# Three seams and the tail of a decoder step's second half: pools for the output projection, gated weight loads, a last product in two halves

## The chip, the core and the metric

The kernel runs on one core of a Trainium2 chip. TensorE (PE) multiplies matrices into PSUM, VectorE (DVE) and ScalarE (ACT) work element by element, GpSimd (POOL) does small vector work here, and SyncE (SP) issues nearly all DMA transfers, in its program order. The metric is the device time of one execution in microseconds; less is better.

## The reference, cut to what matters

One decoder layer runs over 1024 prompt tokens and 64 tokens of eight decoding requests: two attention groups, an output projection, and an MLP, with a norm before and after each half.

```python
def rms_norm(x, g):
    xf = x.astype(jnp.float32)
    y = xf * lax.rsqrt(jnp.mean(xf * xf, axis=-1, keepdims=True) + NORM_EPS)
    return (y * g.astype(jnp.float32)).astype(x.dtype)
...
    mix = jnp.concatenate([o_diff, o_nsa], axis=-1) @ w_out
    x = x + rms_norm(mix, g_post_mix)
    hm = rms_norm(x, g_pre_mlp)
    ff = jnp.square(jax.nn.relu(hm @ w_up)) @ w_down
    x = x + rms_norm(ff, g_post_mlp)
```

`w_out` is 1024 x 1024, `w_up` 1024 x 4096, `w_down` 4096 x 1024, all in float32.

## The kernel before

All of it is one program whose instructions a scheduler puts in order on each engine; every engine then runs its list in that order. Tiles come from pools, memory areas that open and close like brackets; a tile that lies where a closed pool lay waits for that pool's last readers and writers. Each product is made of three fp32r products: a factor is split into a high part (`act_copy`, ACT, L138) and a low part (a subtraction on DVE, L1333 in `split2`), and high x high, low x high and high x low are added in PSUM.

**Differential attention** is the stage before. Its results go transposed to `mixT` in DRAM, one column block per tile of 128 tokens; the last head's last tiles end it.

**Output projection** (`phase_out`, L1232). Eight blocks of `w_out` are loaded into a ring of four tiles `ur` (L1240) and split into tiles `w` (L1245). Token tiles 0 to 7 and tile 8 (the 64 decoding tokens) then each go through `front` (load `mx` from `mixT` and `cx` from x, split `mx` into `mh`), `prod` (two halves of 24 matmuls into PSUM tiles `C`, L1271, three buffers) and `post` (norm, residual into `x1d`, second norm, eight transposes L1296 into `xf`). The pools of this phase are `xca`, `ur`, `w2`, `cc` and `cl` on the left and `xf` on the right.

**MLP up** (`phase_up`, L1366). Both MLP products use Strassen's scheme: seven products for four quarters, in the order `UORD`. `x_factor(i, p)` makes the seven x factors `xc` for each of two column halves p of the tokens (QT = 272 columns each); `factor(j, i)` makes the seven weight factors `us` for a block j. Per j, 168 matmuls (L1398) fill four PSUM tiles `Ua` to `Ud`; from them come seven blocks of h that are stored to `hF` in DRAM (L1418). The last four stores of a block need DVE sums of all its products.

**MLP down** (`phase_down`, L1492). `w_down` is four quarters q of 4 MB, each loaded in four chunks c (L1512). For each of seven factors in the order `DORD` and each of 16 blocks sb (112 steps n), `factor(n)` splits a weight block into `wf`, a block `hr` of `hF` into `hf`, and 24 matmuls (L1573) add into four tiles `Dn`. Four `hr` buffers are loaded ahead (L1506). `later` sets at which steps the chunks of quarters 1, 3 and 2 are issued. `done(i, db)` adds a finished product into the quarters `acc`.

**Finish** (`finish`, L1587). After the last product ten token tiles (five of each token half) are transposed back (L1597), squared and summed on ACT (L1598), scaled on DVE (L1600), added to `x1d` (L1603) and stored (L1608).

Of the kernel before, what the change touches and what calls it, by code (L numbers as in the profile page):

```python
# [17 lines left out]
F32 = mybir.dt.float32  # L18
# [28 lines left out]
DORD = (0, 6, 4, 5, 1, 3, 2)  # L47
# [77 lines left out]
class Kern:  # L125
# [1106 lines left out]
    def phase_out(self, cp, cl):  # L1232
# [5 lines left out]
        for k in range(KC):  # L1238
            raw = self.rp.tile([P, 4, 256], F32, name="ur", bufs=4).rearrange("p a n -> p (a n)")
# [6 lines left out]
            ws.append(w)  # L1246
        gpost = cl.tile([P, D], F32, name="gpost")
# [3 lines left out]
        xins, mhs, pss = {}, {}, {}  # L1251

        def front(t):
            m = self.tok(t)[2]
            xin = xins[t] = cp.tile([P, D], F32, name="cx", bufs=2)
            mx = cp.tile([P, KC, P], F32, name="mx", bufs=1)
            nc.sync.dma_start(mx[:, :, :m], self.mixT[:, t * P:t * P + m].rearrange("(k p) t -> p k t", p=P))
            nc.sync.dma_start(xin[:m], self.xsrc(t))
            mh = mhs[t] = cp.tile([P, 2, KC, P], FR, name="mh", bufs=2)
            self.act_copy(mh[:, 0, :, :m], mx[:, :, :m])  # L1260
            nc.vector.tensor_sub(mh[:, 1, :, :m], mx[:, :, :m], f32(mh[:, 0, :, :m]))
            pss[t] = []
# [41 lines left out]
        for t in range(NT - 1):  # L1304
            front(t)
# [60 lines left out]
    def phase_up(self, wp, tp, psU, close):  # L1366

        nc, A, rp = self.nc, self.A, self.rp
# [12 lines left out]
        def factor(j, i):  # L1381
# [4 lines left out]
            W[j, i] = w = wp.tile([P, 2, 4, P], FR, name="us", bufs=8)  # L1386
# [105 lines left out]
    def phase_down(self, qp, ap, fp, psD):  # L1492
# [5 lines left out]
        quarter, acc, F, R = {}, {}, {}, {}  # L1498
        quarter[0] = qp.tile([P, NB, 512], F32, name="q0")
        HB = 4  # L1500
        hr = [(i, sb) for i in DORD for sb in range(NB)]

        def load_h(n):
            i, sb = hr[n]
            R[n] = self.hp.tile([P, HT], F32, name="hr", bufs=HB)
            nc.sync.dma_start(R[n], self.hF[i, sb * P:sb * P + P])  # L1506

        def load_w(q, c):
            if q not in quarter:
                quarter[q] = qp.tile([P, NB, 512], F32, name=f"q{q}")  # L1510
            r, e = q % 2, q // 2
            nc.sync.dma_start(quarter[q][:, c * 4:c * 4 + 4], w_dn[e, :, c * 4:c * 4 + 4, r * 512:r * 512 + 512])  # L1512


        def factor(n):
            i, sb = hr[n]
            if n + HB < len(hr):
                load_h(n + HB)
            w = fp.tile([P, 2, 512], FR, name="wf", bufs=3)
            a11, a21, a12, a22 = ((quarter[q][:, sb] if q in quarter else None) for q in range(4))  # L1520
# [28 lines left out]
        later = {}  # L1549
        for k, (q, c) in enumerate([(q, c) for q in (1, 3, 2) for c in range(4)]):  # L1550
            later.setdefault(2 + (k % 4) * 4 + (k // 4) * NB, []).append((q, c))
        for c in range(4):
            load_w(0, c)
            load_h(c)
        for k in range(4):
            acc[k] = ap.tile([P, 4, HT], F32, name=f"acc{k}")
        for n in range(2):
            factor(n)
        first = list(range(0, NT, 2)) + [NT]
        for n, (i, sb) in enumerate(hr):  # L1560
            for q, c in later.get(n, ()):
                load_w(q, c)
# [359 lines left out]
```

## Time and profile before

| what | us |
|---|---|
| median of 3 runs | 1874.84 |
| lowest and highest run | 1874.23, 1878.4 |
| the profiled execution, own time | 1880.47 |
| its span, first to last instruction | 1878.7 |
| PE busy | 1717.1 (91% of the span) |
| DVE busy, ACT busy | 1140.6 (61%), 862.3 (46%) |

The profile has a page with shares of the span and of each of its 40 equal slices, a chain of the work that ended last, groups of instructions, and a timeline in which an instruction shows what ended the idle time before it. A busy matmul is a pipelined one, so the cadence of matmuls is read from long unbroken runs, not from the length of one.

### The profile page before, as it was taken

To read this page: it belongs to the slowest core of one execution; us is meant where nothing else is said; L and a number is where in the kernel's file an instruction comes from. 1 tells how busy PE (TensorE), PEld (TensorE's weight loads), DVE (VectorE), ACT (ScalarE), POOL (GpSimd) and SP (SyncE) were. 2 spreads that over 40 slices of the span, in tenths; PEclk is the share of its full clock that TensorE was granted. 3 is DMA by queue.
4 is the path that set the end of the run, shared out by engine and by line. 5 is a ranking of instruction groups with operands and counts; after the bars stand their busy time and mean duration, and the time that the engine had idled before them with its cause. 6 is when DMAs were issued, how large, how long until landed. Compare 5 with 4: busy or idle time off the path is not lost.

```text
span 1878.7 us, 33337 instructions
## 1 busy us (share of the span) xinstructions
PE 1717.1 (91%) x12155; PEld 1496.4 (80%) x12155; DVE 1140.6 (61%) x2673; ACT 862.3 (46%) x2168; POOL 280.5 (15%) x517
## 2 busy tenths in 40 slices
PE   6789999999999999999959969999999569999996
PEld 5778776776657787888747849999999469999995
DVE  4257767667754666666564576666665456448546
ACT  4254446556653555555453444444443224443333
POOL 1133335333321111111100100000000000000002
PEclk8899999999999999999989979999999779999997
DMA  8632000021102524333245304444432853333533
GB/s 167 120 83 47 17 12 21 6 79 51 30 8 58 158 69 138 87 89 112 59 127 174 133 23 128 146 145 138 151 133 104 322 191 91 96 106 91 176 91 110
DMA packets 191600, 191.92 MB, mean 102 GB/s; under 512 B 32291, under 2 KB 148619, under 8 KB 191435
## 3 DMA queue, kind: packets, MB, share of 16 engines
q1 hardware_dynamic: 190138, 187.51, 33.5%
q10 hardware_dynamic: 1296, 2.27, 0.5%
q8 instruction: 96, 1.57, 0.4%
q14 instruction: 70, 0.57, 0.1%
HBM read 133.75 MB, written 55.97 MB: 101 GB/s over the span
## 4 chain that ended last, share of the span: by engine, by line
PE 79%; DVE 6%; DMA 3%; issue 2%; SPq 2%; ACT 1%; POOL 1%; POOLq 0%; ACTq 0%; DVEq 0%
PE Dn L1573 17%; PE M L336 11%; PE C L1271 5%; PE S L409 5%; PE Ua L1398 5%; PE Ub L1398 5%; PE Uc L1398 5%; PE o L501 5%; PE T L516 4%; PE Ud L1398 2%; PE o L613 2%; SPq L1512 1%; PE S L1094 1%; PE o L1219 1%; PE S L336 1%
## 5 line engine op out<-in xcount | busy, mean ns | idle before, releaser
L1573 PE MATMUL Dn<-hf,wf 128*128 128x272 f32 x2688 | 344.4, 291 | 37.8 <-ACT hf L138 37.4
L1573 PEld LDWEIGHTS Dn<-hf,wf 128*128 128x128 f32 x2688 | 343.4, 192 | 38.7 <-ACT hf L138 38.1
L336 PE MATMUL M<-w,xt 128*128 128x384 f32 (+4 forms) x1584 | 296.0, 332 | 13.1 <-ACT nat L138 12.6
L336 PEld LDWEIGHTS M<-w,xt 128*128 128x128 f32 (+1 forms) x1584 | 247.6, 193 | 27.3 <-ACT nat L138 14.0
L426 ACT ACTIVATE p<-S,nm 128x512 f32<-128x512 f32 (+3 forms) x288 | 160.3, 562 | 102.3 <-DVE nm L421 55.5
L174 POOL TENSOR_TENSOR rs_r<-rs_t,mhalf 128x1 f32<-128x1 f32 (+2 forms) x64 | 45.2, 709 | 1011.6 <-DVE rs_t L172 976.8
L417 DVE TENSOR_REDUCE nm<-S 128x1 f32<-128x512 f32 (+3 forms) x288 | 148.1, 527 | 60.0 <-PE S L416 39.1
L409 PE MATMUL S<-kst,qs 128*128 128x512 f32 (+3 forms) x576 | 162.5, 375 | 6.3 <-ACT p L426 5.1
L138 ACT ACTIVATE wf<-q 128x512 fp32r<-128x512 f32 x112 | 70.7, 631 | 211.8 <-PE Dn L1573 196.3
L1333 DVE TENSOR_TENSOR wf<-q,wf 128x512 fp32r<-128x512 f32 x112 | 77.3, 691 | 149.2 <-ACT wf L138 149.1
L1271 PE MATMUL C<-w,mh 128*128 128x512 f32 (+1 forms) x432 | 104.2, 402 | 16.2 <-ACT mh L138 13.6
L480 POOL TENSOR_SCALAR p<-p,coef 128x640 f32<-128x640 f32 (+7 forms) x128 | 93.0, 741 | 146.0 <-DVE coef L477 83.3
L1398 PE MATMUL Ub<-xc,us 128*128 128x272 f32 x768 | 106.3, 291 | 6.4 <-ACT us L138 6.4
L1333 DVE TENSOR_TENSOR us<-ur,us 128x512 fp32r<-128x512 f32 x96 | 66.0, 691 | 74.5 <-ACT us L138 74.5
L1271 PEld LDWEIGHTS C<-w,mh 128*128 128x128 f32 (+1 forms) x432 | 80.2, 187 | 37.1 <-ACT mh L138 13.8
L409 PEld LDWEIGHTS S<-kst,qs 128*128 128x128 f32 x576 | 94.4, 196 | 18.1 <-ACT p L426 7.8
L1398 PE MATMUL Ua<-xc,us 128*128 128x272 f32 x768 | 104.0, 291 | 2.6 <-ACT us L138 1.1
L1398 PEld LDWEIGHTS Ub<-xc,us 128*128 128x128 f32 x768 | 100.8, 190 | 6.9 <-ACT us L138 6.7
L1398 PE MATMUL Uc<-xc,us 128*128 128x272 f32 x768 | 102.8, 289 | 1.9 <-DVE uh L1446 1.6
L1398 PEld LDWEIGHTS Ua<-xc,us 128*128 128x128 f32 x768 | 99.9, 190 | 3.4 <-ACT us L138 1.2
L1398 PEld LDWEIGHTS Uc<-xc,us 128*128 128x128 f32 x768 | 99.1, 189 | 2.4 <-DVE uh L1446 1.8
L138 ACT ACTIVATE us<-ur 128x512 fp32r<-128x512 f32 x96 | 59.9, 628 | 75.3 <-PE Uc L1398 48.4
(306 smaller groups left out, 3048.5 us busy)
## 6 DMA issues: line engine op xcount, KB each, us to landing
hr<-hF SPq DMA_DIRECT2D x112, 272.0 KB
hF<-uh SPq DMA_DIRECT2D x105, 272.0 KB
kvp<-cache_diff_kv SPq DMA_DIRECT2D x128, 128.0 KB
ur<-w_up SPq DMA_DIRECT2D x32, 512.0 KB
q<-w_down SPq DMA_DIRECT2D x16, 1024.0 KB
raw<-w_in SPq DMA_DIRECT2D x32, 192.0 KB
raw<-w_in SPq DMA_DIRECT2D x40, 128.0 KB
xin<-x_prompt SPq DMA_DIRECT2D x8, 512.0 KB
```

Of the source, the lines that this page charges most:

```text
L138: self.nc.scalar.activation(out, in_, AF.Copy, scale=scale)
L336: nc.tensor.matmul(ps[1][:m, :n], self.xt[c][:, a, k, c0:c0 + m], ws[k][:, b, :n], start=i == 0, stop=i == len(ops) - 1)
L409: nc.tensor.matmul(S[:, a * P - lo:b * P - lo], qs[:, ps, j, :], kst[hf][:, kc, a * P - lo:b * P - lo], start=ps == 0, stop=ps == 1 and no ...
L417: nc.vector.reduce_max(nm[:, n:n + 1], S[:, a * P - lo:b * P - lo], axis=AX.X, negate=True)
L426: nc.scalar.activation(p[:, a * P:b * P], tiles[n][:, a * P - lo:b * P - lo], AF.Exp, bias=nm[:, 0:1], accum_out=sums[:, n:n + 1])
L480: nc.gpsimd.tensor_scalar(v, v, coef[:, sw + 1, j:j + 1], 0.0, op0=OP.mult, op1=OP.add)
L501: nc.tensor.matmul(st["o"][half * 64:half * 64 + 64, pr * 256:pr * 256 + 256], lhsT, rhs, start=not started[half], stop=last, skip_group_c ...
L516: nc.tensor.transpose(T[:, m * 256 + jj * P:m * 256 + jj * P + P], st["p", sw, pr * 2 + jj][:, kb * P:(kb + 1) * P], self.ident)
L1271: nc.tensor.matmul(ps[:m], mhs[t][:, a, k, :m], ws[k][:, b, n * 512:n * 512 + 512], start=cnt == 0, stop=cnt == 3 * KC - 1)
L1333: lo.tensor_sub(w[:, 1], src, f32(w[:, 0]))
L1398: nc.tensor.matmul(ps[:, p, :QT], w[:, a, k, :], x[:, b, k, :], start=start and cnt == 0, stop=cnt == 11, skip_group_check=True)
L1573: nc.tensor.matmul(self.dps[db][:, p, :QT], w[:, a, db * P:(db + 1) * P], h[:, b, p * QT:(p + 1) * QT], start=sb == 0 and m == 0, stop=sb ...
```

## The change

**Projection.** The `ur` ring moves into a pool `rr` on the right side, where the last head's weights lay; x and `mixT` tiles share a ring of three tiles `us` there, the split `mh` becomes two tiles `xm`. `xca` and `xf` lie right too, so that `w2` opens where x lay. The first two weights come before `front(0)`, and x is asked for in `prod`. In `phase_up` the factor ring of eight is three tiles of `rr` and five of its own, and two x factors use the `xm` tiles.

**Down.** Each chunk of a quarter is a tile of its own. The first two chunks lie in a pool `qe` on the right; the first two factors are made as their chunks are asked for. A chunk of quarters 1, 3 and 2 first gets a one-column DVE copy from the weight split of its step n (the gate), so its load waits for that. `DORD` ends with 2, 3. The last factor, 3, runs 16 blocks for one half of the token columns and then 16 for the other, with 12 matmuls a step and half-wide `hr` loads; its weight splits are kept in tiles `wl` and used twice. `finish` of the five tiles `T1` (whose quarters are final after factor 2) is placed in the first half, two tiles of `T0` in the second, three after the end.

```diff
-DORD = (0, 6, 4, 5, 1, 3, 2)
+DORD = (0, 6, 4, 5, 1, 2, 3)
...
-    def phase_out(self, cp, cl):
+    def phase_out(self, cl):
...
-        for k in range(KC):
-            raw = self.rp.tile([P, 4, 256], F32, name="ur", bufs=4).rearrange("p a n -> p (a n)")
+        rr = self.rr
+
+        def weight(k):
+            raw = rr.tile([P, 4, 256], F32, name="ur", bufs=4).rearrange("p a n -> p (a n)")
...
+        def front(t):
+            m = self.tok(t)[2]
+            mx = rr.tile([P, 2, 4, P], F32, name="us", bufs=3).rearrange("p a b n -> p (a b) n")
+            nc.sync.dma_start(mx[:, :, :m], self.mixT[:, t * P:t * P + m].rearrange("(k p) t -> p k t", p=P))
+            mh = rr.tile([P, 2, 4, QT], FR, name="xm", bufs=2).rearrange("p a b n -> p (a b n)")[:, :2 * KC * P]
...
+        for k in range(2):
+            weight(k)
+        front(0)
+        for k in range(2, KC):
+            weight(k)
+        for i in UORD[:5]:
+            self.xtile(self.xca, i, 0)
...
+            if n == 0:
+                xins[t] = rr.tile([P, 2, 4, P], F32, name="us", bufs=3).rearrange("p a b n -> p (a b n)")
+                nc.sync.dma_start(xins[t][:m], self.xsrc(t))
...
-            W[j, i] = w = wp.tile([P, 2, 4, P], FR, name="us", bufs=8)
+            n = len(W) % 8
+            W[j, i] = w = (self.rr if n < 3 else wp).tile([P, 2, 4, P], FR, name="us", bufs=3 if n < 3 else 5)
...
-    def phase_down(self, qp, ap, fp, psD):
+    def phase_down(self, qe, qp, fp, psD):
...
-        hr = [(i, sb) for i in DORD for sb in range(NB)]
+        last = DORD[-1]
+        hr = [(i, sb, None) for i in DORD[:-1] for sb in range(NB)] + [(last, sb, p) for p in range(2) for sb in range(NB)]
...
+        def load_w(q, c, gate=None):
+            early = q == 0 and c < 2
+            t = quarter[q, c] = (qe if early else qp).tile([P, 4, 512], F32, name="qe" if early else f"q{q}{c}",
+                                                           bufs=2 if early else 1)
+            if gate is not None:
+                nc.vector.tensor_copy(t[:, 0, 0:1], gate)
             r, e = q % 2, q // 2
-            nc.sync.dma_start(quarter[q][:, c * 4:c * 4 + 4], w_dn[e, :, c * 4:c * 4 + 4, r * 512:r * 512 + 512])
+            nc.sync.dma_start(t, w_dn[e, :, c * 4:c * 4 + 4, r * 512:r * 512 + 512])
...
+            if i != last:
+                w = fp.tile([P, 2, 512], FR, name="wf", bufs=3)
+            elif p == 0:
...
+                    wl[sb // 2] = qp.tile([P, 2, 2, 512], FR, name=f"q{1 + sb // 8}{sb // 2 % 4}")
+                w = wl[sb // 2][:, sb % 2]
+            else:
+                w = wl[sb // 2][:, sb % 2]
+            if p != 1:
+                self.split2(w, {0: a11, 6: a11, 4: a21, 5: a11, 1: a12, 3: a22, 2: a12}[i], v)
...
-            for q, c in later.get(n, ()):
-                load_w(q, c)
-            if n + 2 < len(hr):
-                factor(n + 2)
+            if n in gate:
+                load_w(*gate[n], gate=f32(F[n][0][:, 1, 0:1]))
+            factor(n + 2)
...
+                o = dps[db // 2][:, db % 2, :QT]
+                for m, (a, b) in enumerate(((0, 0), (1, 0), (0, 1))):
+                    nc.tensor.matmul(o, w[:, a, db * P:(db + 1) * P], h[:, b, :], start=st and m == 0,
+                                     stop=sp and m == 2)
+                if sp:
+                    d = acc[1][:, db, p * QT:(p + 1) * QT]
+                    nc.vector.tensor_add(d, o, d)
+            if p == 0 and sb % 3 == 2:
+                finish(T1[sb // 3])
+            if p == 1 and sb in (5, 9):
+                finish(T0[sb // 8])
+        for t in T0[2:]:
+            finish(t)
```

What the scheduler makes of it on the engines' lists is read at three places. In each row stands the line, the operation, out <- in, the size, and how many follow one another.

**PE, from the attention's last tiles into the projection.** `T<-ident,p` and `o<-vst,pt` are the transposes and value products of a token tile of the last head, `T<-ident,jk` the transpose of its result, `C` the projection. Before:

```order
L602 MATMUL T<-ident,p 128x128 x7
L613 MATMUL o<-vst,pt 128x128 x7
L564 MATMUL T<-ident,jk 128x128
L602 MATMUL T<-ident,p 128x128 x8
L613 MATMUL o<-vst,pt 128x128 x8
L564 MATMUL T<-ident,jk 128x128
L1271 MATMUL C<-w,mh 128x512 x109
```

And now:

```order
L613 MATMUL o<-vst,pt 128x128 x7
L1284 MATMUL C<-w,xm 128x512 x26
L564 MATMUL T<-ident,jk 128x128
L602 MATMUL T<-ident,p 128x128 x4
L1284 MATMUL C<-w,xm 128x512 x19
L602 MATMUL T<-ident,p 128x128 x4
L613 MATMUL o<-vst,pt 128x128 x4
L1284 MATMUL C<-w,xm 128x512 x18
L613 MATMUL o<-vst,pt 128x128 x4
L1284 MATMUL C<-w,xm 128x512 x9
L564 MATMUL T<-ident,jk 128x128
L1284 MATMUL C<-w,xm 128x512 x30
```

72 projection matmuls (tile 0, and the first half of tile 1) now stand ahead of the attention's last transpose.

**SP, from MLP up into MLP down.** `hF<-uh` are the stores of h, `hr<-hF` its loads, `q` and `qe` the chunks of `w_down`. Before:

```order
L1512 DMA q_17549<-w_down 128x4x512
L1506 DMA hr<-hF 128x544
L1512 DMA q_17549<-w_down 128x4x512
L1506 DMA hr<-hF 128x544
L1512 DMA q_17549<-w_down 128x4x512
L1418 DMA hF<-uh 128x544 x2
L1506 DMA hr<-hF 128x544
L1418 DMA hF<-uh 128x544 x2
L1512 DMA q_17650<-w_down 128x4x512 x4
L1512 DMA q_18179<-w_down 128x4x512 x4
L1512 DMA q_18720<-w_down 128x4x512 x4
L1506 DMA hr<-hF 128x544 x80
```

And now:

```order
L1433 DMA hF<-uh 128x544 x23
L1534 DMA qe<-w_down 128x4x512 x2
L1433 DMA hF<-uh 128x544 x4
L1525 DMA hr<-hF 128x544 x4
L1534 DMA q_17563<-w_down 128x4x512
L1534 DMA q_17567<-w_down 128x4x512
L1534 DMA q_17645<-w_down 128x4x512
L1525 DMA hr<-hF 128x544 x7
L1534 DMA q_17776<-w_down 128x4x512
L1525 DMA hr<-hF 128x544 x4
L1534 DMA q_17907<-w_down 128x4x512
L1525 DMA hr<-hF 128x544 x4
```

The block of twelve chunk loads is spread, one for every four `hr`; the first `hr` moves behind the last four stores of h.

**PE, the start of the last factor.** `q_20743` and the like are the kept splits `wl`, `acc` the finished quarters that are transposed back. Before, all products come first:

```order
L1573 MATMUL Dn<-hf,wf 128x272 x2688
L1597 MATMUL Dn<-ident,acc_17562 128x128 x4
L1597 MATMUL Dn<-ident,acc_17563 128x128 x4
L1597 MATMUL Dn<-ident,acc_17562 128x128 x4
L1597 MATMUL Dn<-ident,acc_17563 128x128 x4
```

And now:

```order
L1628 MATMUL Dn<-hf,wf 128x272 x2304
L1638 MATMUL Dn<-hf,q_20743 128x272 x24
L1638 MATMUL Dn<-hf,q_20810 128x272 x4
L1661 MATMUL Dn<-ident,acc_17574 128x128 x2
L1638 MATMUL Dn<-hf,q_20810 128x272 x8
L1661 MATMUL Dn<-ident,acc_17574 128x128 x2
L1661 MATMUL Dn<-ident,acc_17573 128x128 x4
L1638 MATMUL Dn<-hf,q_20810 128x272 x12
L1638 MATMUL Dn<-hf,q_20851 128x272 x24
```

The transposes of finished tiles stand between the steps of the last factor. On ACT and DVE the splits `wl` are spread over the two factors before it.

## Rows read from the trace of the kernel before

**Rows 1.** The page's 40 slices of 47 us: busy tenths of PE.
```profile
PE   6789999999999999999959969999999569999996
```

**Rows 2.** Chain that ended last: start us, us, what ran without a break.
```profile
1040.51 10.90 PE C L1271 x48
...
1519.08 179.86 PE Dn L1573 x1416
```

**Rows 3.** Stretches: us, PE, PEld, DVE, ACT, POOL busy (count), PE clock, DMA share, GB/s.
```profile
950.00:960.00 10.00, 7.21 (x36) 5.27 (x34) 6.68 (x16) 5.14 (x17) 0.78 (x2) 0.83 0.48 158
960.00:970.00 10.00, 4.44 (x31) 3.43 (x32) 4.90 (x14) 5.83 (x19) 1.09 (x2) 1.00 0.02 7
970.00:980.00 10.00, 4.25 (x21) 3.55 (x21) 4.35 (x9) 6.27 (x14) 0.55 (x1) 0.73 0.18 53
980.00:990.00 10.00, 0.00 (x0) 0.00 (x0) 6.14 (x10) 5.50 (x9) 0.00 (x0) 0.50 0.96 316
```

**Rows 4.** Groups of 950 to 990 us: busy us, mean ns | idle before.
```profile
L1245 DVE TENSOR_TENSOR w<-ur,w 128x512 fp32r<-128x512 f32 x16 | 10.1, 686 | 3.1 <-ACT w L138 3.1
L138 ACT ACTIVATE w<-ur 128x512 fp32r<-128x512 f32 x16 | 8.9, 618 | 4.6 <-DMA ur<-w_out 4.6
```

**Rows 5.** Timeline into the projection: start us, us, instruction [idle before <-releaser].
```profile
940.55 5.37 SPq L1240 DMA_DIRECT2D ur<-w_out  x4
...
964.30 1.83 PE L613 MATMUL o<-vst,pt 128*128 128x128 f32 x14 [0.21 <-ACT pt L138]
...
970.65 3.40 PE L613 MATMUL o<-vst,pt 128*128 128x128 f32 x16
...
990.20 13.18 PE L1271 MATMUL C<-w,mh 128*128 128x512 f32 x47 [13.60 <-ACT mh L138]
```

**Rows 6.** Timeline from the projection into MLP up.
```profile
1094.22 7.19 PE L1271 MATMUL C<-w,mh 128*64 128x512 f32 x24 [2.64 <-DVE ctmp L1286]
...
1107.94 1.28 DVE L1291 SCALAR_TENSOR_TENSOR ctmp<-cx,rs_r,gpre 64x1024 f32<-64x1024 f32 x1 [0.72 <-POOL rs_r L174]
...
1109.14 2.48 DVE L1333 TENSOR_TENSOR xc<-xf,xc 128x1088 fp32r<-128x1088 f32 x2
...
1130.81 1.77 PE L1398 MATMUL Ua<-xc,us 128*128 128x272 f32 x12 [0.87 <-ACT uh L138]
```

**Rows 7.** Timeline from MLP up into MLP down.
```profile
1461.43 3.29 PE L1398 MATMUL Uc<-xc,us 128*128 128x272 f32 x24 [1.57 <-DVE uh L1446]
...
1468.81 3.13 SPq L1418 DMA_DIRECT2D hF<-uh  x2
...
1471.50 5.40 PE L1573 MATMUL Dn<-hf,wf 128*128 128x272 f32 x24 [6.78 <-ACT hf L138]
...
1476.85 28.95 SPq L1512 DMA_DIRECT2D q<-w_down  x12
...
1485.07 11.54 PE L1573 MATMUL Dn<-hf,wf 128*128 128x272 f32 x72 [8.16 <-ACT hf L138]
...
1498.67 2.50 DVE L1525 TENSOR_TENSOR q<-q,q 128x512 f32<-128x512 f32 x4 [2.96 <-DMA q<-w_down]
...
1518.37 2.10 ACT L138 ACTIVATE hf<-hr 128x544 fp32r<-128x544 f32 x3 [21.11 <-DMA hr<-hF]
...
1519.08 11.13 PE L1573 MATMUL Dn<-hf,wf 128*128 128x272 f32 x69 [22.48 <-ACT hf L138]
```

**Rows 8.** A stretch within that seam.
```profile
1490.00:1500.00 10.00, 6.60 (x53) 6.38 (x51) 4.94 (x9) 1.90 (x3) 0.00 (x0) 1.00 1.05 385
```

**Rows 9.** Timeline of the tail.
```profile
1846.70 3.65 PE L1597 MATMUL Dn<-ident,acc 128*128 128x128 f32 x32
...
1849.73 1.28 DVE L1600 SCALAR_TENSOR_TENSOR q<-Dn,rs_r,q 128x1024 f32<-128x1024 f32 x1 [0.66 <-POOL rs_r L174]
...
1873.32 1.27 DVE L1600 SCALAR_TENSOR_TENSOR q<-Dn,rs_r,q 32x1024 f32<-32x1024 f32 x1 [0.44 <-POOL rs_r L174]
...
1875.87 0.33 SPq L1608 DMA_DIRECT2D o_y_s<-q  x1
```

More of the change, by code (lines that the diff above doesn't have):

```diff
@@ L1304, in phase_out @@
         for t in range(NT - 1):
-            front(t)
+            if t:
+                front(t)
             prod(t, 0)
@@ L1547, in done, with fin @@
                 nc.vector.tensor_add(d, c, d)
-        later = {}
+        def fin(n):
+            if n < 4:
+                room[n] = None
+            if room[n % 4] is None or n >= 4:
+                room[n % 4] = qe.tile([P, 4, 512], F32, name="qe", bufs=2) if n % 4 < 2 else \
+                    qp.tile([P, 4, 512], F32, name=f"q0{n % 4}")
+            return room[n % 4]
+        room = {}
+        gate = {}
         for k, (q, c) in enumerate([(q, c) for q in (1, 3, 2) for c in range(4)]):
-            later.setdefault(2 + (k % 4) * 4 + (k // 4) * NB, []).append((q, c))
+            gate[2 + (k % 4) * 4 + (k // 4) * NB] = (q, c)
         for c in range(4):
@@ L1554, in phase_down @@
             load_h(c)
+            if c < 2:
+                factor(c)
         for k in range(4):
[L1556 to L1560, printed above, removed]
-            for q, c in later.get(n, ()):
-                load_w(q, c)
-            if n + 2 < len(hr):
-                factor(n + 2)
-            w, h = F.pop(n)
-            for db in range(4):
-                if sb == 0:
-                    if db == 0:
-                        self.dps = {}
-                    self.dps[db] = psD.tile([P, 2, 512], F32, name="Dn", tag="Dn")
-                for p in range(2):
-                    for m, (a, b) in enumerate(((0, 0), (1, 0), (0, 1))):
-                        nc.tensor.matmul(self.dps[db][:, p, :QT], w[:, a, db * P:(db + 1) * P],
-                                         h[:, b, p * QT:(p + 1) * QT], start=sb == 0 and m == 0,
-                                         stop=sb == NB - 1 and m == 2)
-                if sb == NB - 1:
-                    done(i, db)
@@ L1579, in phase_down @@
-        fin = [qp.tile([P, 8, D], F32, name=f"q{q}") for q in range(2)]
-        gp = fin[1][:, 0]
-        nc.scalar.dma_start(gp, A["g_post_mlp"].to_broadcast([P, D]))
-        for n, t in enumerate(first):
-            self.finish(fin, n, psD, gp, t, (acc[0], acc[1]))
-        for n, t in enumerate(list(range(1, NT, 2)) + [NT + 1]):
-            self.finish(fin, n + 5, psD, gp, t, (acc[3], acc[2]))
-    def finish(self, fin, n, psD, gp, t, acc):
+            acc[k] = qp.tile([P, 4, HT], F32, name=f"acc{k}")
@@ L1588, in finish @@
+        for t in T0[2:]:
+            finish(t)
+    def finish(self, room, fs, psD, gp, t, acc):
         nc, A = self.nc, self.A
         m, c0, r0 = (32, HT - 32, SEQ + 32 * (t - NT)) if t >= NT else (P, t // 2 * P, t * P)
-        x1 = fin[0][:, n % 8]
+        room = room.rearrange("p a n -> p (a n)")
+        x1 = room[:, 0:D]
         nc.sync.dma_start(x1[:m], self.x1d[r0:r0 + m])
-        tmp = fin[1][:, 1 + n % 7].rearrange("p (a n) -> p a n", a=2)
-        ss = self.fs.tile([P, 1], F32, name="fss", bufs=2)
+        tmp = room[:, D:2 * D].rearrange("p (a n) -> p a n", a=2)
+        ss = fs.tile([P, 1], F32, name="fss", bufs=2)
```

118 lines of the change are left out of this document (74 added, 44 removed).

## The prediction

> **What bounds the kernel now.** I began with the page's row of 40 slices [rows 1]: PE is at nine tenths or more from the fifth slice on, except in four places, slices 21 (939 to 986 us), 24 (1080 to 1127), 32 and 33 (1456 to 1550) and the last one. The reader is to see that the kernel is bound by PE, and that what can be won lies in those four dips, not in the busy share of any other engine. The chain of waits gives the price of PE's own work where nothing interrupts it [rows 2]: 48 projection matmuls take 10.90 us (0.227 each), 1416 of MLP down take 179.86 (0.127 each). I then read each dip in the timeline. The change touches all four, so the sum has four terms. It is made against the profiled execution, 1880.47 us with a span of 1878.7, and carried over to the median of 1874.84, which is 5.6 lower.
>
> **A. Into the projection.** Before: from 950 to 990 us PE is busy 7.2, 4.4, 4.3 and 0 of every 10 us [rows 3]. ACT and DVE split the weights of w_out only after the attention's last tile, so PE waits 13.60 us and starts at 990.20, at a low clock: the granted clock of the stretch before is 0.50, that is 1.2 GHz, after 10 idle us, and 47 matmuls take 13.18 us where 10.7 would do [rows 3, 5]. The second half of tile 1 (after 72 matmuls) so starts at 990.20 + 13.18 + 25 x 0.227 = 1009.1.
>
> After: the first loads already went out at 940.55 [rows 5], what held the splits back was where the weight tiles lay, and that is gone. The 72 matmuls stand between the attention's last operations. The price is that 16 splits and two of the mixT tile come into the attention's last tiles: DVE 10.1 [rows 4] plus two of about 1.2 (twice the elements of a split's 686 ns, nearly), 12.5 us in all, ACT 8.9 plus 2.1. DVE is idle 8.4 us in 950 to 970 [rows 3], so the attention's chain slides by the missing 4.1; I take 5. The value products of the last tile but one ended at 966.1, so the 72 start at 971 and need 16.3; the last tile's value products (3.40) and transposes (eight of 0.114 [rows 9]) lie between them: 992 [rows 5]. Then comes a new wait: the next half needs a PSUM buffer of tile 0, and its squares stand on ACT behind the attention's last result. The same wait costs 2.64 where only one square is missing [rows 6]; with two squares and the gain load behind it I take 5. So 997 plus 2 for the low clock: 999 against 1009.1, a gain of **10**. Ends: 3 if the chain slides by all 12.5, 20 if it doesn't slide and the pause is 2.6.
>
> **B. From the projection into MLP up.** After the last token tile is normed (1107.94), DVE has the x factors, the sums and the weight factors one after the other from 1109.14 on, and PE runs without a break only from 1130.81, with 48 matmuls done by then [rows 6]. In the new order two x factors, a weight factor and two weight sums, some 4.4 us at half of the pair's 2.48 and about 0.65 for the small ones, come ahead of that tile's norm; the two x factors delay the norm by about 2.5. DVE so ends about as late as before, but what PE needs first comes first: about 96 matmuls are done by then, 48 x 0.127 = 6 more. I take a gain of **5**; ends -2 (only the delayed norm counts) and 8.
>
> **C. From MLP up into MLP down.** Before: the last up product ends at 1464.7; the first two pieces, 24 and 72 matmuls, wait 6.78 and 8.16, and then PE waits 22.48 until 1519.08, because hr loads stand on SP behind twelve chunk loads that take SP 28.95 us from 1476.85 and the DMA engines run at 385 GB/s meanwhile [rows 7, 8]. ACT's wait for that hr is 21.11 [rows 7]. The fifth step starts at 1519.08, and 69 matmuls at first at the low clock take 11.13 for 8.8: as good as 1521.4.
>
> After: the twelve are spread, 1 MB for four hr of 0.28 MB, 2.1 MB in four steps of 3.05 us, 173 GB/s. But the first hr stands behind the last four stores of h, whose first two went out from 1468.81 [rows 7]. Ahead of it and with it go 3.5 MB (two chunks, four stores, itself), from 1465 at 385 GB/s 9.1 us, with some 1.5 to start (a small last store takes 2.8 [rows 9]), 1475.5; two splits, 1.4: PE starts at 1477, not 1471.5. 48 matmuls, half of them at the low clock (5.40 for 24 [rows 7]), end at 1485.5. The third step then waits, since DVE has the four subtractions with the first chunk of quarter 1 (2.50 a chunk [rows 7]) ahead of its split: that chunk lands after 4.5 MB more (three hr, three chunks, the row of gains), 11.7 us, at 1487.2, so the step starts at 1490.5 and the fifth at 1497, with low clock 1499. Gain 1521.4 - 1499 = **22**. Ends: 15 if half of the chunks still collide, 27 if the third step doesn't wait.
>
> The rate decides this. The trace shows 385 GB/s over 10 us in this seam [rows 8]. The Trainium skill (DMA: Bandwidth & Descriptors, Specifications) gives about 358 GB/s as the HBM limit of one core; the trace differs and decides. By the page the 8 MB would take 1.5 us longer and the gain would be 20.5.
>
> **D. Last factor and tail.** Before: from the first scaling at 1849.73 to the tenth at 1873.32 there are nine steps of 2.62 us; the last store goes out at 1875.87 and the span ends 2.8 later [rows 9]. With three tiles left seven steps fall away: 18.3. In their place seven tiles' transposes, and some of the other three, stand between the products: 66 x 0.114 (32 take 3.65 [rows 9]) = 7.5 on PE. The matmuls stay 384, 12 for each of 32 half steps of 1.52 us. DVE's weight splits of this factor are moved into the two factors before, where it has room; per three half steps it has then three half splits of 0.4 and one tile of 2.62, 3.8 of PE's 4.6 plus 0.9. For PSUM waits at the two joints I take 2.3. Gain 18.3 - 7.5 - 2.3 = **8.5**; ends 2 (a wait of 0.2 at each half step) and 13. The gates themselves, twelve copies of one column, cost DVE below 0.2 each beside PE's steps: nothing. The x1 loads and the stores lie beside the products.
>
> **Sum.** 10 + 5 + 22 + 8.5 = 45.5: 1880.5 becomes 1835, and the median 1874.84 becomes **1829**.
>
> **Rivals.**
> - *The front doesn't pay.* ACT and DVE run their lists in order, and a split put ahead of the attention's exponentials holds up the chain that PE waits for. For it: DVE and ACT are busy 49 to 67% of 950 to 970. Against it: DVE's 8.4 idle us there [rows 3]. A gives 3, B nothing: 1841.
> - *The gate is a new wait.* DVE's subtractions wait for a chunk whose load waits for DVE: if each of twelve chunks costs 1 us beyond the lead of two steps, C gives 10: 1841. Against it: a chunk needs 2.7 us at 385 GB/s, the lead is some 6.
> - *More than that.* No slide in A, B at 8, C at 25, D at 11: 1813.
> - *Slower.* The halves double the hr loads to 32, and on SP they stand behind the stores of finished tiles, which wait for DVE. If each half step waits for a whole load, then a transfer of 2.8 [rows 9] and two half splits, 3.5 us, take the place of 1.52: 32 x 2.0 = 64 us, 1893. It decides from 1.4 us per half step. For it: PE did wait 22.48 us for hr behind other transfers on SP [rows 7]. The Trainium skill (TensorE: Matmul & The Clock Gate, The mechanism) says that matmuls run strictly in order, so a transpose or product that waits holds all behind it; no row here shows one overtaking. Against it: four hr are loaded ahead, 6 us.
> - *Nothing changes*, if what is won in C and D is lost at the joints.
>
> **Chances.** Forecast 0.62 (its own range 1816 to 1841), front 0.12, gate 0.10, more 0.08, slower 0.05, nothing 0.03. The first four are faster: 0.92. A measurement of this kernel tells about 0.2%, 3.7 us, from no change. The range that holds 8 in 10, with both partial cases and most of the good one, is 1812 to 1850.
>
> **What would show it.** A: projection matmuls before the attention's last transpose, first at 968 to 975, then one pause of 3 to 6 us before the 73rd. B: PE without a break from about 1130 less A, with some 96 matmuls done. C: no wait of 20 us for hr; waits before the first and the third step, the fifth starting some 33 us after the last up product. D: a tail of 13 to 14 us after the last product, and about 60 us for the last factor. The forecast is wrong if the first projection matmul starts after 980, if a wait for a chunk recurs with every gate, or if PE falls below nine tenths in the last factor.

## The result, and the profile after

| | before | after |
|---|---|---|
| median of 4 runs, us | 1876.12 | 1845.36 |
| range | 1874.23 to 1878.40 | 1841.84 to 1847.84 |
| ratio, 95% interval | | 0.9835 [0.9814, 0.9855] |
| profiled execution, its span | 1880.47, 1878.7 | 1843.10, 1841.3 |

30.8 us less by the medians; predicted were 45.5. The two profiled executions differ by 37.4, but 6.1 of that lie ahead of everything the change touches: the last long run of matmuls before the first seam begins at 938.09 in the one trace and at 931.97 in the other. The chains (start us, us, what), before and after:

```profile
938.09 3.30 PE M L336 x19
```
```profile
931.97 3.29 PE M L336 x19
```

So all places below are counted from that start. From there to the end of the span it is 940.6 us before and 909.3 after, 31.3 less, which agrees with the medians. The row of slices, against [rows 1], has the same four dips, each shallower; the second now takes two slices:

```profile
PE   6789999999999999999989977999999699999997
```

**Into the projection.** Stretches (us, busy of PE, PEld, DVE, ACT, POOL, PE clock, DMA share, GB/s), to be held against [rows 3]:

```profile
940.00:950.00 10.00, 5.16 (x35) 3.70 (x34) 9.52 (x26) 8.53 (x23) 1.92 (x4) 0.91 0.95 338
950.00:960.00 10.00, 8.21 (x29) 5.94 (x29) 9.04 (x20) 8.31 (x23) 0.72 (x1) 0.58 1.08 371
...
990.00:1000.00 10.00, 7.54 (x26) 6.04 (x27) 4.39 (x7) 2.43 (x8) 1.10 (x2) 0.83 0.38 128
```

DVE is full from 940 on, and the attention slides, as the prediction said. Then the timeline and the chain of the projection:

```profile
968.51 6.39 PE L1284 MATMUL C<-w,xm 128*128 128x512 f32 x26
...
992.46 2.85 PE L1284 MATMUL C<-w,xm 128*128 128x512 f32 x6 [3.59 <-DVE ctmp L1299]
```
```profile
992.46 8.81 PE C L1284 x30
...
1014.45 11.20 PE C L1284 x48
```

The 73rd matmul starts 60.5 us from the common start, before 70.8 (1008.9 in that trace): 10.3 gained. But the next 30 run at a granted clock of 0.83 and take 8.81 where 7.0 would do, and each 48 take 11.20 where before the change they took 10.90 [rows 2].

**Into MLP up.** After 48 matmuls PE stands still. What it waits for is ACT's copy of the first product, and that copy waits for DVE:

```profile
1107.42 1.17 PE L1413 MATMUL Ub<-xc,us 128*128 128x272 f32 x8
...
1119.93 0.40 ACT L138 ACTIVATE uh<-Ua 128x272 f32<-128x272 f32 x1 [3.57 <-DVE xc L1347]
...
1120.38 3.09 PE L1413 MATMUL Ua<-xc,us 128*128 128x272 f32 x12 [11.79 <-ACT uh L138]
```

Before, PE also had 48 matmuls done where it began to run on, at 1130.81 [rows 6].

**Into MLP down, and through it.**

```profile
1454.44 1.68 PE L1413 MATMUL Uc<-xm,us 128*128 128x272 f32 x12
...
1459.04 2.47 SPq L1433 DMA_DIRECT2D hF<-uh  x4
...
1461.57 4.69 SPq L1525 DMA_DIRECT2D hr<-hF  x4
...
1466.70 2.82 SPq L1534 DMA_DIRECT2D q<-w_down  x3
...
1470.45 7.79 PE L1628 MATMUL Dn<-hf,wf 128*128 128x272 f32 x48 [14.33 <-ACT hf L138]
1471.18 0.66 ACT L138 ACTIVATE hf<-hr 128x544 fp32r<-128x544 f32 x1 [0.78 <-DMA hr<-hF]
1471.19 21.62 SPq L1525 DMA_DIRECT2D hr<-hF  x7
...
1480.08 2.50 DVE L1546 TENSOR_TENSOR qe<-qe,q 128x512 f32<-128x512 f32 x4 [0.44 <-DMA q<-w_down]
1480.73 1.94 ACT L138 ACTIVATE hf<-hr 128x544 fp32r<-128x544 f32 x3 [1.82 <-DMA hr<-hF]
...
1481.44 30.78 PE L1628 MATMUL Dn<-hf,wf 128*128 128x272 f32 x222 [3.19 <-ACT hf L138]
```

The wait of 22.48 [rows 7] is gone; there are two, of 14.33 and 3.19. The second is for the hr of the third step. Making the first two factors also asks for the hr four steps ahead (`load_h(n + HB)` in `factor`), so the four tiles of the ring go to steps 1, 5, 2 and 6, and the second step's split is released by the third of these four loads (1471.18). The third step's hr goes out only when the first split has freed a tile, at 1471.19, behind three chunks, and lands at 1480.73.

Farther on DVE waits for chunks (engine, line, releaser, us in all, times, longest; 1530 to 1700 us), and PE loses 1.73 us of 70:

```profile
DVE q L1548 <- DMA q<-w_down: 7.5, 4, 3.4
```
```profile
1530.00:1600.00 70.00, 68.27 (x539) 67.43 (x538) 51.40 (x87) 31.49 (x54) 0.00 (x0) 1.00 0.56 183
```

**Tail.** The last factor begins at 1770.31, its last product ends at 1827.15, and the last store goes out at 1838.43 [rows 9 for before]:

```profile
1770.31 3.65 PE L1638 MATMUL Dn<-hf,q 128*128 128x272 f32 x28
...
1826.53 0.62 PE L1638 MATMUL Dn<-hf,q 128*128 128x272 f32 x3
...
1838.43 0.33 SPq L1672 DMA_DIRECT2D o_y_s<-qe  x1
```

### The profile page after: what moved, and what is told of

It is laid out like the page before. It is cut to its first block, busy times and chain, and to the rows that moved or that the text cites. A ratio compares the mean times of both kernels' runs of the same rounds, so it can differ in the third digit from the quotient of the medians.

```text
span 1841.3 us, 33377 instructions
## 1 busy us (share of the span) xinstructions
PE 1716.2 (93%) x12155; PEld 1495.9 (81%) x12155; DVE 1140.5 (62%) x2705; ACT 865.1 (47%) x2184; POOL 275.2 (15%) x517
## 4 chain that ended last, share of the span: by engine, by line
PE 80%; DVE 6%; DMA 4%; issue 2%; ACT 2%; POOL 1%; SPq 0%; DVEq 0%; POOLq 0%; ACTq 0%
PE Dn L1628 13%; PE M L336 12%; PE C L1284 6%; PE S L409 5%; PE Ua L1413 5%; PE Ub L1413 5%; PE Uc L1413 5%; PE o L501 5%; PE T L516 4%; PE Dn L1638 3%; PE Ud L1413 3%; PE o L613 2%; PE S L1094 1%; PE o L1219 1%; DMA q<-w_down 1%
## 5 line engine op out<-in xcount | busy, mean ns | idle before, releaser
L1628 PE MATMUL Dn<-hf,wf 128*128 128x272 f32 x2304 | 294.8, 291 | 19.6 <-ACT hf L138 17.5
L1628 PEld LDWEIGHTS Dn<-hf,wf 128*128 128x128 f32 x2304 | 293.3, 191 | 21.1 <-ACT hf L138 18.0
L336 PE MATMUL M<-w,xt 128*128 128x384 f32 (+4 forms) x1584 | 295.7, 332 | 12.7 <-ACT nat L138 12.1
L174 POOL TENSOR_TENSOR rs_r<-rs_t,mhalf 128x1 f32<-128x1 f32 (+2 forms) x64 | 39.5, 619 | 981.8 <-DVE rs_t L172 978.9
L409 PE MATMUL S<-kst,qs 128*128 128x512 f32 (+3 forms) x576 | 163.1, 375 | 7.9 <-ACT p L426 7.5
L1284 PE MATMUL C<-w,xm 128*128 128x512 f32 (+1 forms) x432 | 107.1, 406 | 6.2 <-DVE ctmp L1299 6.2
L409 PEld LDWEIGHTS S<-kst,qs 128*128 128x128 f32 x576 | 94.4, 195 | 19.8 <-ACT p L426 10.4
L138 ACT ACTIVATE wf<-q 128x512 fp32r<-128x512 f32 x72 | 45.5, 632 | 123.2 <-PE Dn L1628 115.7
L1284 PEld LDWEIGHTS C<-w,xm 128*128 128x128 f32 (+1 forms) x432 | 79.5, 187 | 29.0 <-DVE ctmp L1299 6.9
L138 ACT ACTIVATE hf<-hr 128x544 fp32r<-128x544 f32 (+1 forms) x128 | 75.4, 590 | 43.5 <-PE Dn L1638 29.2
L1347 DVE TENSOR_TENSOR hf<-hr,hf 128x544 fp32r<-128x544 f32 (+1 forms) x128 | 82.5, 648 | 18.8 <-ACT hf L138 18.7
L149 DVE COPY pt<-T 128x512 f32<-128x512 f32 (+3 forms) x100 | 61.7, 619 | 49.7 <-PE T L516 34.7
```

The source lines that it names most:

```text
L138: self.nc.scalar.activation(out, in_, AF.Copy, scale=scale)
L336: nc.tensor.matmul(ps[1][:m, :n], self.xt[c][:, a, k, c0:c0 + m], ws[k][:, b, :n], start=i == 0, stop=i == len(ops) - 1)
L409: nc.tensor.matmul(S[:, a * P - lo:b * P - lo], qs[:, ps, j, :], kst[hf][:, kc, a * P - lo:b * P - lo], start=ps == 0, stop=ps == 1 and no ...
L1284: nc.tensor.matmul(ps[:m], mhs[t][:, a, k, :m], ws[k][:, b, n * 512:n * 512 + 512], start=cnt == 0, stop=cnt == 3 * KC - 1)
L1347: lo.tensor_sub(w[:, 1], src, f32(w[:, 0]))
L1628: nc.tensor.matmul(dps[db][:, q, :QT], w[:, a, db * P:(db + 1) * P], h[:, b, q * QT:(q + 1) * QT], start=st and m == 0, stop=sp and m == 2)
```

## Experiments

All kernels in one table: median and ratio to the kernel before run beside it, and, of the profiled execution, the us from the common start to five places of the timeline. Kernels without the halves have no row of their own for the start of the last factor. For them it is the end of the last product less 384 matmuls of 0.1256 (24 take 3.015 in an undisturbed step); before, 1846.9 less 48.2 is 1798.7.

| kernel | median | ratio [95%] | last C ends | last U ends | first Dn | last factor | end |
|---|---|---|---|---|---|---|---|
| before | 1876.12 | | 163.3 | 526.6 | 533.4 | 860.6 | 940.6 |
| after | 1845.36 | 0.9835 [0.9814, 0.9855] | 156.7 | 524.2 | 538.5 | 838.3 | 909.3 |
| front_only | 1864.86 | 0.9940 [0.9924, 0.9957] | 156.5 | 524.0 | 537.9 | 849.0 | 929.2 |
| down_only | 1845.04 | 0.9834 [0.9818, 0.9851] | 163.1 | 526.4 | 545.5 | 841.0 | 912.0 |
| uh_room | 1843.39 | 0.9823 [0.9807, 0.9839] | 156.5 | 518.9 | 532.9 | 835.2 | 906.3 |
| no_gate | 1862.35 | 0.9932 [0.9915, 0.9949] | 156.4 | 523.8 | 538.1 | 854.8 | 925.9 |
| hr_early | 1833.87 | 0.9777 [0.9760, 0.9793] | 156.7 | 524.2 | 532.2 | 826.5 | 897.6 |
| late_subs | 1841.46 | 0.9831 [0.9802, 0.9860] | 156.3 | 523.7 | 537.8 | 834.9 | 905.9 |
| whole_last | 1856.49 | 0.9897 [0.9881, 0.9914] | 156.2 | 523.5 | 538.3 | 839.8 | 923.3 |
| three_mends | 1828.13 | 0.9745 [0.9725, 0.9766] | 159.2 | 521.6 | 529.7 | 822.0 | 893.0 |
| loads_in_up | 1819.65 | 0.9696 [0.9681, 0.9711] | 156.9 | 522.0 | 521.8 | 812.3 | 883.6 |
| after_again | 1847.07 | 0.9837 [0.9824, 0.9851] | 156.2 | 523.6 | 539.4 | 839.7 | 910.7 |
| down_again | 1848.31 | 0.9852 [0.9836, 0.9867] | 159.5 | 522.8 | 542.4 | 837.0 | 908.0 |
| mh_left (one run) | 1839.92 | | 155.1 | 521.7 | 531.9 | 834.7 | 905.8 |

**1. The front alone, and MLP down alone.** front_only is the changed kernel with the MLP down, its pools and DORD of before; down_only is the kernel before with those of the change. The edit of front_only (down_only has it the other way round):

```diff
-            with self.pool("qe", side="right") as qe, self.pool("qd") as qp, ...
-                self.phase_down(qe, qp, fp, psD)
+            with self.pool("qd") as qp, self.pool("hr") as self.hp, self.pool("acc") as ap, ...
+                self.phase_down(qp, ap, fp, psD)
```

> The changed projection and MLP up with the MLP down of before. By the landmarks of the two profiled executions the front gained 16.6 us at the 73rd projection matmul, 12.7 at the last one and 8.6 at the last up product. Theory (the four seams add up): 8 to 9 us less than the kernel before, the 73rd matmul near 992, PE without a break in MLP up near 1120, and the old wait of some 22 us for hr in MLP down. Rival (what the front wins is lost in the next seam, since MLP down's loads are what the end waits for): within 3 us of the kernel before.

> The projection and MLP up of before with the changed MLP down. Theory (the seams add up): gain of 22 at the seam, less 3 for four waits for chunks, plus 9 in the tail: 27 to 30 us less than the kernel before. Rival (the early chunks and the hr loads find a free queue only because the new pools end MLP up otherwise): the first hr lands 5 us or more later than in the changed kernel and the gain is under 23.

Alone they give 10.4 (1875.22 beside them) and 30.2 us, together 30.8: they do not add up. The 16.6, 12.7 and 8.6 of the expectation hold the 6.1 us that lie ahead of the change; from the common start they are 10.3, 6.6 and 2.5. At the last up product front_only is only 2.6 us ahead of before. The rest of its gain comes inside the old MLP down:

```profile
1452.06 1.37 SPq L1521 DMA_DIRECT2D hr<-hF  x3
...
1459.57 1.59 SPq L1521 DMA_DIRECT2D hr<-hF  x3
...
1464.19 36.23 SPq L1527 DMA_DIRECT2D q<-w_down  x16
...
1472.06 23.03 PE L1588 MATMUL Dn<-hf,wf 128*128 128x272 f32 x168 [13.91 <-ACT wf L138]
...
1513.38 6.79 PE L1588 MATMUL Dn<-hf,wf 128*128 128x272 f32 x40 [18.30 <-ACT hf L138]
```

Six hr go out before the sixteen chunks, so seven steps (168 matmuls) are done ahead of the long wait, and not four as before [rows 7]. That gain the new MLP down has anyway. The first theory, that the seams add up, holds for down_only (predicted 27 to 30) and falls for what is left of the front beside it. The rival for down_only had a part of it: its first down product does stand 19.1 us after the last up product, against 14.3 in the changed kernel. But no second wait follows, and the fifth step starts 34.1 us after the last up product there and 34.2 in the changed kernel, so the gain stays.

**2. Is the front worth anything beside the new MLP down?** Both kernels once more, with more runs.

> The changed kernel once more beside its MLP down alone, in more rounds, to tell what the changed projection is worth on top of the changed MLP down. Theory (the landmarks of one execution each: 2.5 us ahead at the last up product, 2.7 at the end): 2 to 3 us less than with MLP down alone. Rival (the medians of the first runs, 1845.4 and 1845.0): within 1 us of it.

> The projection and MLP up of before with the changed MLP down, in more rounds. Theory: 2 to 3 us more than the changed kernel; rival: within 1 us of it.

1.2 us apart by the medians, with overlapping intervals, and 2.7 the other way at the end of the profiled executions (908.0 against 910.7); in the first pair the medians were 0.3 apart against the front and the ends 2.7 for it. The difference lies in the old projection, whose last C ends at 163.1 in one execution and at 159.5 in the other. A worth of the front beside the new MLP down is not shown; if there is one, it is within some 3 us.

**3. The wait in MLP up.** Four result tiles get room of their own:

```diff
             def stile():
+                if j == 0 and pq == (0,) and len(self.early) < 4:
+                    self.early.append(self.ue.tile([P, 1, QT], F32, name=f"ue{len(self.early)}"))
+                    return self.early[-1]
                 return self.sp.tile([P, 2, QT], F32, name="uh", bufs=13)[:, :n]
...
```

> The changed kernel, with room of their own for the first four result tiles of MLP up (uh), which otherwise lie where xf lay and so must wait until the last x factor has been read. Theory (PE's 11.8 us of waiting in MLP up come from the copy of the first product, which stands on ACT behind the x factors for want of room): PE runs on after 48 matmuls, at least 24 more are done by 1112, the low clock after the pause goes too: 3 to 7 us less than the changed kernel. Rival (DVE's list of x factors to 1119.7 is the bound, and PE would wait for the factors themselves): within 1.5 us of the changed kernel, with the same pause ended by DVE.

```profile
1111.29 1.67 PE L1413 MATMUL Ua<-xc,us 128*128 128x272 f32 x12
...
1116.54 1.79 PE L1413 MATMUL Ub<-xc,us 128*128 128x272 f32 x12 [1.31 <-DVE ue L1451]
...
1120.50 2.16 PE L1413 MATMUL Ub<-xc,us 128*128 128x272 f32 x12 [2.17 <-DVE ue L1459]
...
1125.15 3.06 PE L1413 MATMUL Uc<-xc,us 128*128 128x272 f32 x12 [2.49 <-DVE uh L1464]
```

The pause of 11.79 is gone, three of 1.3 to 2.5 for DVE's sums remain, and the last up product ends 5.3 us sooner: the wait was one for room. Both theories hold a part. Of the 5.3 MLP down gives 2.3 back; the median, 2.0 less, is within the interval of the changed kernel.

**4. Without the gates.**

```diff
-                load_w(*gate[n], gate=f32(F[n][0][:, 1, 0:1]))
+                load_w(*gate[n])
```

> The changed kernel without the twelve one-column copies that tie a load of a later chunk of w_down to a step. Theory (the gates are what keeps hr from standing behind chunks): the twelve chunks go out nearly in a row again, 12.6 MB at 385 GB/s, 33 us; the hr of the seventh step lands near 1500 instead of before 1494, and PE waits some 8 us more in all (5 to 20): 1850 to 1865. Rival (the gain at this seam comes from the early chunks and the order of the first hr alone, and the gates only bring DVE's waits for chunks): no later than the changed kernel, down to 3 us less.

```profile
1470.84 0.34 SPq L1525 DMA_DIRECT2D hr<-hF  x1
1471.30 11.26 SPq L1534 DMA_DIRECT2D q<-w_down  x5
...
1482.66 2.83 SPq L1525 DMA_DIRECT2D hr<-hF  x1
1485.53 14.09 SPq L1534 DMA_DIRECT2D q<-w_down  x6
1496.70 11.11 PE L1628 MATMUL Dn<-hf,wf 128*128 128x272 f32 x72 [9.52 <-ACT hf L138]
1499.72 16.44 SPq L1525 DMA_DIRECT2D hr<-hF  x7
1513.73 6.49 PE L1628 MATMUL Dn<-hf,wf 128*128 128x272 f32 x35 [5.92 <-ACT hf L138]
```

17.0 us more, in the upper half of the expected 5 to 20. Without a data dependence the loads go out as soon as there is room, ahead of the hr of later steps. The gates are what the gain in MLP down rests on: from the last up product to the last factor it takes 331.0 us without them, 314.1 with them, and 334.0 before the change.

**5. The waits for chunks.** Late in the new MLP down DVE's subtractions stand right behind the chunk they need, some 20 us before their result is used. Here they are held back by six steps:

```diff
             factor(n + 2)
+            if n - 6 in gate and n - 6 >= NB:
+                t = quarter[gate[n - 6]][:, :, 0]
+                nc.vector.scalar_tensor_tensor(t, f32(F[n][0][:, 1, 0:4]), 0.0, t, op0=OP.mult, op1=OP.add)
             w, h = F.pop(n)
```

> The changed kernel with the subtractions of quarters 3 and 2 tied to a step six after the gate of their chunk, by adding zero times a weight factor to one column of the chunk (0.15 us of DVE each). Theory (DVE's four waits of 1.9 to 3.4 us for chunks, 7.5 in all between 1530 and 1600, come from the place of the subtractions in DVE's list, some 6 us behind the gate and 20 us before they are needed): the waits for chunks there fall below 2 us in all, PE runs on through 1535 to 1600, 2 to 3 us less than the changed kernel. Rival (the chunks come so late that any step would wait): the waits stay above 5 us and the time within 1 us.

```profile
1530.00:1600.00 70.00, 70.00 (x561) 70.00 (x560) 53.44 (x94) 32.80 (x56) 0.00 (x0) 1.00 0.56 187
```

PE is never idle in that stretch, and DVE waits for no chunk in it. From the last up product to the last factor it takes 311.2 us, in the changed kernel 314.2: 3.0 less. The median's 3.9 less has an interval that reaches over the changed kernel's.

**6. The last factor over full width.**

```diff
-        hr = [(i, sb, None) for i in DORD[:-1] for sb in range(NB)] + [(last, sb, p) for p in range(2) ...]
+        hr = [(i, sb, None) for i in DORD for sb in range(NB)]
...
-        for t in T0[2:]:
+        for t in T1 + T0:
             finish(t)
```

> The changed kernel with the last quarter product over full width and all ten tiles finished after it. Theory (the tail is what the halves save, and they cost only the transposes): from the start of the last factor to the end 80 us as before the change instead of 70.8: 8 to 10 us more than the changed kernel. Rival (the halves cost PE as much in PSUM and split waits as the tail gives): under 4 us more.

11.1 us more by the medians, 14.0 from the common start, of which 1.5 lie ahead of the last factor. From there to the end it takes 83.5 us (expected 80) and in the changed kernel 71.0. Its tail, from the end of the last product to the end of the span, is 35.3 us, and 31.8 before: four rooms serve ten tiles, so work on a tile waits until a store has left its room (once 3.7 us). Without that 3.5, which is not the halves' doing, they are worth some 9 of the 12.5 us.

**7. hr sooner.** The hr tiles get a pool on the right:

```diff
-            R[n] = qp.tile([P, HT], F32, name="hr", bufs=HB)
+            R[n] = self.hp.tile([P, HT], F32, name="hr", bufs=HB)
...
-            with self.pool("qe", side="right") as qe, self.pool("qd") as qp, ...
+            with self.pool("qe", side="right") as qe, self.pool("hr", side="right") as self.hp, self.pool("qd") as qp, ...
```

> The changed kernel with the four hr tiles of MLP down in a pool of their own on the right, beside the early chunks, where MLP up's weight factors lay. Four hr and the two early chunks then stand on SP ahead of the last four stores of h. Theory (PE's 14.3 us between the last up product and the first down product are the first hr standing behind those stores and chunks): PE starts 3 to 6 us after the last up product and has six steps in hand while three chunks land: 7 to 11 us less than the changed kernel. Rival (the early start is given back, since the chunks of quarter 0 and 1 set when the later steps can run): a new wait of 5 us or more before the seventh step, gain under 4.

```profile
1459.15 1.04 SPq L1525 DMA_DIRECT2D hr<-hF  x2
...
1462.76 2.77 SPq L1433 DMA_DIRECT2D hF<-uh  x4
...
1466.77 22.09 PE L1628 MATMUL Dn<-hf,wf 128*128 128x272 f32 x152 [8.08 <-ACT hf L138]
...
1467.72 3.76 SPq L1525 DMA_DIRECT2D hr<-hF  x2
...
1471.52 2.90 SPq L1534 DMA_DIRECT2D q<-w_down  x3
...
1489.32 50.85 PE L1628 MATMUL Dn<-hf,wf 128*128 128x272 f32 x404 [0.47 <-DVE hf L1347]
```

The stores now stand behind the first four hr. The first wait is 8.08 in place of 14.33 (3 to 6 were expected), that of the third step is gone, and nothing of 5 us comes later: 11.5 us less, a little more than expected. So hr behind the stores, as the prediction had put it, was 6.3 of the first wait. The third step no longer waits since its hr now goes out ahead of the three chunks (1467.72 and 1471.52) and not behind them. Loading the hr in the order of the steps, and changing nothing else, was not tried. The 8.08 left are taken up in experiment 9.

**8. Together.** uh_room, late_subs and hr_early in one kernel:

> Room of its own for uh, the hr tiles on the right and the late subtractions together. Theory (the three places are independent): the sum of their gains, 2 for uh, 7 to 11 for hr, 2 to 3 for the subtractions: 11 to 16 us less than the changed kernel, 1830 to 1834. Rival (a gain of one is given back at the next, as the room for uh gave back 2.3 of its 5.3 us in MLP down): under 9.

17.2 us less than the changed kernel (11 to 16 were expected); the three alone give 2.0, 3.9 and 11.5, together 17.4. From the common start it is 16.3 against 3.0, 3.4 and 11.7; in this execution the last C ends 2.5 us later than in the changed kernel. As far as these runs can tell, the three are independent.

**9. MLP down's first loads inside MLP up.** To this the right pool stays open over MLP down; its ur and us tiles take the first loads, ahead of the last block's products, and its xm tiles two of the sums:

```diff
+            if j == NJ - 1:
+                self.down_loads()
...
+    def down_loads(self):
...
+        for u in range(4):
+            t = self.half().rearrange("p (s c) -> p s c", s=2)
+            nc.sync.dma_start(t, w[0, :, 2 * u:2 * u + 2, 0:512])
...
+            if u < 3:
+                h = self.hrow()
+                nc.sync.dma_start(h, self.hF[DORD[0], u * P:u * P + P])
...
```

> The three mends, and MLP down's first loads put into MLP up: half of quarter 0 goes into the four ur tiles and three hr into the three us tiles of the right pool, which stays open, before the products of MLP up's last block; two sums lie in its xm tiles; the ring of hr has three tiles instead of four. Theory (the 8.1 us that PE still waits between the last up product and the first down product, and the low clock behind them, are loads issued only as MLP up ends): PE waits under 3 us there and 5 to 9 us less than the three mends in all, 1819 to 1823. Rival (the transfers only move, and the three hr tiles or the next chunks hold the steps up): a new wait of 5 us or more in the first twelve steps, gain under 3.

```profile
1452.15 2.62 PE L1413 MATMUL Uc<-xm,us 128*128 128x272 f32 x12
1454.61 21.19 PE L1654 MATMUL Dn<-hf,wf 128*128 128x272 f32 x168
1476.05 1.27 PE L1654 MATMUL Dn<-hf,wf 128*128 128x272 f32 x8 [0.25 <-ACT hf L138]
1477.79 122.39 PE L1654 MATMUL Dn<-hf,wf 128*128 128x272 f32 x975 [0.47 <-DVE hf L1347]
```

The last up product and the first down product follow each other without a gap, and two waits under 0.5 are left. 8.5 us less than the three mends; 1819.65 is 25.7 below the changed kernel and 57.2 below the kernel before beside it (1876.8). This is the version that beats both. It changes more than the moment of the loads: the first hr also come in the order of the steps, and their ring has three tiles; what each is worth by itself was not tried.

**10. Why do the projection's matmuls take longer?** The split mixT tiles, their stationary operand, get tiles on the left:

```diff
-            mh = rr.tile([P, 2, 4, QT], FR, name="xm", bufs=2).rearrange("p a b n -> p (a b n)")[:, :2 * KC * P]
-            mh = mhs[t] = mh.rearrange("p (a k n) -> p a k n", a=2, k=KC)
+            mh = mhs[t] = cl.tile([P, 2, KC, P], FR, name="mh", bufs=2)
...
```

The two x factors of MLP up that used the xm tiles get tiles of their own as well.

> The changed kernel with the split mixT tiles (the matmuls' stationary operand) in a pool of their own on the left instead of in the xm tiles on the right. One look. In the changed kernel 48 projection matmuls without a break take 11.44 us, before 11.15. Theory (the place of the stationary operand sets this): 11.15 again and 2 us come back over the seven tiles. Rival (it is something else: the weights' place, or what ACT and DVE do beside them): 11.44.

```profile
1016.01 11.16 PE L1283 MATMUL C<-w,mh 128*128 128x512 f32 x48
```

11.16 in place of 11.44 (the same view of the changed kernel), so it is the place of that operand. In unbroken runs the starts of two projection matmuls are 233 ns apart in all ten traces with the operand in xm, and 227 in all four with it in tiles of its own. The order of instructions in the seam changed too (the first projection matmul comes 9 us later), and one run can't tell the whole time.

## Why the prediction was right, and where it was wrong

The direction and the range held (1845.4 in 1812 to 1850); the forecast's own range, 1816 to 1841, did not. By the common start the four terms came out as 6.6, -4.1, 19.8 and 9.0, sum 31.3, where 10, 5, 22 and 8.5 stood. Of the 14.2 us that are missing 9.1 are the second term.

- **A, 10: right in mechanism, 6.6 in size.** The 73rd matmul was to start 12 us sooner, or 10 with the low clock behind it; it came 10.3 sooner, 8.5 with the clock (30 matmuls in 8.81 for 7.0). The attention slid by 8.5 us, more than the 5 taken (first projection matmul 36.5 us from the common start, predicted 32.9), the pause was shorter (3.59 for 5). Another 2 went in the projection itself: 48 matmuls cost 0.3 more for the new place of their operand (experiment 10), while the prediction priced them by the row of the old tiles. The 6.6 is the difference of two executions: the old projection's last C ends at 163.3 and 163.1 in two and at 159.5 in a third, and against that one the new projection gains 3.
- **B, +5: wrong in sign, -4.1.** From the last C to the last up product it is 363.3 us in all three executions of the old projection and some 367.4 in seven of the new one. "What PE needs first comes first: about 96 matmuls are done by then." The first 48 do end some 15 us sooner from the common start. The step failed behind them: the next matmuls write over a product that must first be copied out, and the tile for that copy lies where xf lay until DVE has read the last x factor. Experiment 3 took this wait away and the last up product came 5.3 sooner. The pause also brought the low clock: the 24 matmuls behind it take 5.6 us at a granted clock of 0.53, before 3.3. In the kernel before the same wait stood in [rows 6] as 0.87, last in a row of others, and looked like nothing.
- **C, 22: right in size; 22.5 at the seam, 19.8 at the last factor.** First product 14.3 after the last up product (predicted 12.3), third step 25.3 (25.8), the fifth 34.2 (34.3), with the low clock paid in the third (a granted clock of 0.50 through all of it); in the kernel before the fifth starts at 54.4 and pays 2.3 for the low clock then, so 56.7 counts. The price of the transfers by 385 GB/s and the order on SP carried this. The third step's time came out by another wait than the one named: the prediction had PE wait for DVE's split behind the subtractions, whose chunk came at 1480.08, but what releases PE is ACT's split of an hr that stood behind three chunks and landed at 1480.73. That the time agrees is luck: the chunk came 1.5 us later than predicted (24.0 after the last up product for 22.5), and PE did not wait for the split behind it. The gates were costed at nothing; they cost some 2.7, by DVE's waits for chunks (experiment 5), since the subtractions moved up in DVE's list with the loads. The rival of the gate as a new wait was right in kind, and a quarter in size.
- **D, 8.5: right, 9.0.** Tail 14.1 after the last product (13 to 14 predicted), last factor 56.8 (60), of which 48.2 are its matmuls, 7.6 the 67 transposes in it and 0.9 waits, where 2.3 had been taken. Experiment 6 gives the same worth, some 9.
- **The rivals.** Nearest came that the front doesn't pay (0.12, 1841): the front is 2.5 us ahead at the last up product. Its mechanism, a chain held up by the splits, was a part of it: the attention slid by 8.5 of the 12.5 us that the splits take on DVE. The rest is that the front arrived and gave its lead back, at matmuls, clock and room. The slower rival fell: 0.9 us of waits in 32 half steps, where it needed 1.4 in each.

## What to carry to other kernels

A stage that comes sooner is worth only what the next one can take up: after moving work forward, look for the tile that the next step writes to and ask whose room it lies in, since a wait of 0.87 us can stand for one of 12. A ring of tiles is filled in the order in which the program asks for them: loads asked for ahead can hold the tile that a nearer step needs. Count a gain at every later seam, from a point that both traces share, not at the seam where it is made. Loads that a schedule may move should be tied by a dependence to the step before which they are not wanted, and the work on their data as well, and a stage's first loads belong ahead of the last stores of the one before it.

## What the runs showed of the hardware

- The stationary operand's place changes what a matmul costs: 48 of 128x512 take 11.44 us from the xm tiles and 11.15 from tiles of their own, 6 ns each, with the same shapes and the granted clock at 1.00. Within a partition both kinds of tile are laid out alike (the edit of experiment 10), so it is where the operand lies; what about the place matters was not tried.
- One kernel's seam is not alike in two executions: with the projection of before, the last C ends 163.1 us from the common start in one (down_only) and 159.5 in another (down_again). In these two the last 24 matmuls took 7.26 and 5.74 us after the same wait of 2.64.

```profile
1087.51 7.26 PE L1271 MATMUL C<-w,mh 128*64 128x512 f32 x24 [2.64 <-DVE ctmp L1286]
```
```profile
1086.31 5.74 PE L1271 MATMUL C<-w,mh 128*64 128x512 f32 x24 [2.64 <-DVE ctmp L1286]
```

- The transfers of this core reach 398 GB/s over 10 us in the changed kernel's seam into MLP down. The Trainium skill (DMA: Bandwidth & Descriptors, Specifications) gives about 358 GB/s as one core's HBM limit; the trace differs, and decides. The same page of the Trainium skill (Bandwidth) puts that figure to two cores streaming at once and has more for one alone, with which the trace agrees; what the neighbour core did is not in these runs.

```profile
1466.00:1476.00 10.00, 5.55 (x32) 5.55 (x33) 1.51 (x3) 1.95 (x3) 0.00 (x0) 0.61 1.04 398
```
